# A decoder layer that reads its input transposed as well, with the gates' products ahead of the first norm's row

## The chip, the cores and the metric

The kernel runs on one core of a Trainium2 chip. The metric is the device time of one execution in microseconds (us). Three executions of the kernel before took 700.8, 701.33 and 701.66 us; the median is 701.33 us. Engines: TensorE (PE, its weight loads PEld) multiplies, VectorE (DVE), ScalarE (ACT) and GpSimd (POOL) do the rest, SyncE (SP) and ACT issue DMAs.

## What is computed

One layer of a decoder on x of 256 tokens by 1024 columns. In the reference's words, cut:

```python
xn = rmsnorm(h, mix_norm_g)          # x * rsqrt(mean(x*x) + eps) * g
proj = xn @ w_in                     # aq ak av | mq mk mv mo | mi mf | ga gm
ya = moba_attention(aq, ak, av)
qk = silu(causal_dwconv(concat(mq, mk), conv_w) + conv_b)
ym = mlstm_chunkwise(q, k, mv, mi + b, mf + b)   # gates i, f: 4 heads each
h = h + (sigmoid(ga) * (ya @ w_up_attn) + sigmoid(gm) * (ym @ w_up_mlstm)) @ w_out
h = h + hierarchical_moe(rmsnorm(h))             # 32 experts, top 2 per token
h = rmsnorm(h + (p @ w_ple_proj) * sigmoid(rmsnorm(h) @ w_ple_gate))
```

The change touches only what comes first: the norm of x, the projections mq, mi and mf, mk and aq, and the small vectors (gains, biases, the convolution's weights).

## The kernel before

All arithmetic is 32-bit. A large product is made of three of TensorE's fast kind: each operand is split into a rounded part (`whi`, written by ACT) and the rest (`wlo`, written by DVE: operand minus `whi`), and hi*hi, hi*lo and lo*hi are summed in PSUM. So every 128x512 piece of a weight costs ACT one pass, DVE one pass and TensorE 12 products of 128x256. The pieces pass through three staging buffers (`whi`, `wlo`), later two more (`spare`), so ACT may run up to three pieces ahead of TensorE. The tokens' scale 1/rms is not multiplied into x: the products use x times the gain, and the scale is applied to the results (`rT`, the scales as a row on every partition).

Weights arrive by DMA in 2 MB slots of a ring of ten; XT (x transposed, split, 8 blocks of 128 columns), RW, QK and VV hold results in slots of the same ring. A slot is refilled when its last reader is done. After the front come 32 experts of 6 MB each through the same ring, then a gate product and the last norm.

The start: SP issues x in two halves (L76) between the four 512 KB pieces of the mq weights (L77), then six small vectors, each into some rows of one tile (L92), the gates' weights and biases (L100 to L103), and then the 2 MB weights mk, aq, ak, av, mv, mo (L108). Each DMA uses one of eight completion counters in turn, and its issue waits until the DMA that had that counter before has landed. TensorE runs NWARM0 = 3 products on the identity (L231, `pw`), transposes x with 16 products (L257, `pt`), and for each block k of x runs 12 products into `pmq` (L308 to L310). ACT writes XT and `whi` (L299, L305), DVE their rests (L300, L306), and ACT sums the squares of x in four passes among them (L278). The row `rT` is made from the scales by two transposes (L285, `prt`) ahead of block 6. Then follow a transpose of the small vectors (L246, `pcol`), the gates' 24 products into `pif` (L331 to L333), the chain of small operations on the gates (L396 to L410, `scratch`), the transposes of its result (L416, `pam`), and the products of mk and aq (L331 to L333, `po`), whose results DVE scales by `rT` (L543, L548, L372). The convolution (L362 to L368) follows on ACT and DVE.

The Tile framework orders the instructions on each engine when the program is built; each engine then runs its own in that order, and `after(a, b)` adds an edge that puts a behind b on its engine.

Of the kernel before, what the change touches and what calls it, by code (L numbers as in the profile page):

```python
# [8 lines left out]
F32 = mybir.dt.float32  # L9
# [9 lines left out]
P = 128  # L19
T = 256  # L20
NB = 2
# [13 lines left out]
NWARM0 = 3  # L35
# [13 lines left out]
def layer(ctx: ExitStack, tc: tile.TileContext, A, dbg=None):  # L49
# [13 lines left out]


# [15 lines left out]
    rows = fc.tile([76, P], F32, name="rows")  # L80
    col_of = {}
    r0 = 0
    for nm, src in (
            ("g2", A["ffn_norm_g"].rearrange("o (k p) -> (o k) p", p=P)),
            ("g3", A["ple_norm_g"].rearrange("o (k p) -> (o k) p", p=P)),
            ("cb", A["conv_b"].rearrange("o (k p) -> (o k) p", p=P)),
            ("cw", A["conv_w"].rearrange("o c (k p) -> (o c k) p", p=P)),
            ("gml", A["mlstm_norm_g"].rearrange("o (k p) -> (o k) p", p=P)),
            ("bg", A["b_gate"].rearrange("o (k p) -> (o k) p", p=P)),
    ):  # L90
        n = src.shape[0]
        nc.sync.dma_start(out=rows[r0:r0 + n], in_=src)  # L92
        col_of[nm] = r0
        r0 += n

    wif = fc.tile([P, KD, 8], F32, name="wif")
    ifb = fc.tile([36, 1], F32, name="ifb")

    def load_if():
        nc.sync.dma_start(out=wif, in_=A["w_if"])  # L100
        ifb_v = A["mlstm_if_b"].rearrange("o n -> n o")
        nc.sync.dma_start(out=ifb[0:4], in_=ifb_v[0:4])
        nc.sync.dma_start(out=ifb[32:36], in_=ifb_v[4:8])  # L103
# [13 lines left out]
    first_act = nc.scalar.activation(identb, ident, AF.Copy)  # L117
# [20 lines left out]
    for nm in ("mk", "aq", "ak", "av", "mv", "mo"):  # L138
        wts[nm] = load_cols(A["w_mix"][MIX.index(nm)])
# [66 lines left out]
    def load_router():  # L206
# [6 lines left out]
        nc.sync.dma_start(out=rb[:, 0:NG], in_=A["router_group_b"].to_broadcast([P, NG]))  # L213
        nc.sync.dma_start(out=rb[:, 8:], in_=A["router_expert_b"].to_broadcast([P, NE]))
# [29 lines left out]
    def load_columns():  # L244
        pcol = psf.tile([P, 512], F32, name="pcol", tag="tp")
        nc.tensor.transpose(pcol[:, 0:76], rows, ident[0:76, 0:76])  # L246
        nc.vector.tensor_copy(out=cols, in_=pcol[:, 0:76])
        nc.vector.tensor_scalar(bgh, cols[:, col_of["bg"]:col_of["bg"] + 16], 0.5, None, op0=OP.mult)

# [3 lines left out]
    def transpose_x(k):  # L253
        pt = psf.tile([P, 2, T], F32, name="pt", tag="tp")
        for kk in range(2):
            for b in range(NB):
                after(nc.tensor.transpose(pt[:, kk, b * P:(b + 1) * P], h[:, b, (k + kk) * P:(k + kk + 1) * P], ident),  # L257
                      warm0)
        return pt

    ss = small.tile([P, 2, NB], F32, name="ss", bufs=1)
# [3 lines left out]
    seq = {"act": first_act, "dve": g1_copy}  # L265
# [5 lines left out]
    def on_dve(ins):  # L271
        after(ins, seq["dve"])
        seq["dve"] = ins

    def square_x(i):
        for b in range(NB):
            cs = slice(i * 512, (i + 1) * 512)
            on_act(nc.scalar.activation(y[:, b, cs], h[:, b, cs], AF.Square, accum_out=ss[:, i, b:b + 1]))  # L278

    def norm_x():  # L280
        nc.vector.tensor_tensor(ss[:, 0], ss[:, 0], ss[:, 1], op=OP.add)
        rstd_of(r1[:, 0:NB], ss[:, 0], D, NB)
        prt = psf.tile([P, 512], F32, name="prt", tag="at", bufs=3)
        for b in range(NB):
            nc.tensor.transpose(prt[:, b * P:(b + 1) * P], r1[:, b:b + 1].to_broadcast([P, P]), ident)  # L285
        nc.vector.tensor_copy(out=rT, in_=prt[:, 0:T])
        nc.vector.tensor_scalar(r1[:, 2:4], r1[:, 0:NB], 0.5, None, op0=OP.mult)

    pts = {}
    for k in range(KD):  # L290
        if k in (0, 2, 3):
            for kt in {0: (0, 2), 2: (4,), 3: (6,)}[k]:
                pts[kt] = transpose_x(kt)
# [810 lines left out]
```

## Time and profile before

| | us |
|---|---|
| median of three executions | 701.33 |
| the profiled execution | 701.26 |
| its span, first to last instruction | 699.6 |
| outside the span | 1.66 |
| TensorE busy in the span | 556.4 |
| DVE busy | 279.4 |
| ACT busy | 187.4 |
| mean granted clock of TensorE | 0.925 |

Busy time is a mean over stages with different limits. The front (0 to about 220 us) is one stage, the experts (to about 660 us) another, the end a third; what a change in the front is worth has to be read there, and then followed to the end.

### The profile page before, as it was taken

The page shows a single profiled execution, that of the slowest core. Times are in us where ns is not written, and L with a number is a line of the kernel's source. Part 1 is how long each engine was busy: PE and PEld are TensorE (multiplying, and loading weights), DVE is VectorE, ACT ScalarE, POOL GpSimd, SP SyncE. Part 2 cuts the span into 40 slices and gives each one's busy share as a digit, 9 for nine tenths or more (in the row PEclk, how much of TensorE's full clock was granted, in tenths as well). Part 3 has the DMA queues.
Part 4 walks back from the last instruction along what each step waited for, and adds up shares of the span by engine and source line. Part 5 has one row for each costly group of instructions (what it writes and reads, how often), then busy time and mean ns, then how long its engine had stood idle before and what let it go on. Part 6 is the DMA issues. An engine that isn't in the chain of part 4 may idle for free.

```text
span 699.6 us, 12231 instructions
## 1 busy us (share of the span) xinstructions
PE 556.4 (80%) x5165; PEld 378.1 (54%) x5165; DVE 279.4 (40%) x685; ACT 187.4 (27%) x426; POOL 34.6 (5%) x56
## 2 busy tenths in 40 slices
PE   7899999999999998595566655967656985865895
PEld 6799778899986554252233222634323442432374
DVE  5898667676665333041122015313211230310174
ACT  6575556465453211000000000010000210000164
POOL 3000000001300000000000000000000000000061
PEclk9999999999999999799799787999978997798999
DMA  7956533338787799999999999999999999999911
GB/s 257 430 221 260 219 122 121 121 121 331 301 340 301 316 430 421 433 423 428 427 425 429 426 429 421 427 428 422 430 425 425 424 427 427 428 426 427 412 63 61
DMA packets 21993, 241.49 MB, mean 345 GB/s; under 512 B 4694, under 2 KB 5290, under 8 KB 6955
## 3 DMA queue, kind: packets, MB, share of 16 engines
q1 hardware_dynamic: 21770, 240.37, 82.9%
q8 instruction: 42, 0.69, 0.4%
q10 hardware_dynamic: 160, 0.27, 0.1%
q14 instruction: 21, 0.16, 0.1%
HBM read 239.58 MB, written 1.05 MB: 344 GB/s over the span
## 4 chain that ended last, share of the span: by engine, by line
DMA 49%; PE 44%; DVE 3%; ACT 2%; issue 2%; POOL 1%; POOLq 0%; DVEq 0%; ACTq 0%; SPq 0%
DMA wt<-in_expert_gu 37%; DMA wt<-in_expert_down 11%; PE pg L811 5%; PE po L331 4%; PE po L333 4%; PE po L332 4%; PE po L348 2%; PE po L347 2%; PE po L349 2%; PE px L762 2%; PE pd L828 2%; PE ps L840 2%; PE ps L924 1%; PE pyy L471 1%; PE G L1014 1%
## 5 line engine op out<-in xcount | busy, mean ns | idle before, releaser
L811 PE MATMUL pg<-wt,xe 128*32 128x256 f32 x2032 | 150.6, 431 | 72.5 <-DMA wt<-in_expert_gu 72.5
L811 PEld LDWEIGHTS pg<-wt,xe 128*32 128x32 f32 x2032 | 72.2, 120 | 136.2 <-DMA wt<-in_expert_gu 54.8
L828 PE MATMUL pd<-wt,hT 128*32 128x256 f32 x1024 | 75.4, 443 | 22.0 <-DMA wt<-in_expert_down 17.9
L834 DVE COPY eo<-pd 32x256 f32<-32x256 f32 x64 | 27.1, 423 | 112.7 <-ACT eo L836 112.6
L828 PEld LDWEIGHTS pd<-wt,hT 128*32 128x32 f32 x1024 | 38.7, 124 | 47.4 <-issue 33.3
L836 ACT ACTIVATE eo<-pd 32x256 f32<-32x256 f32 x64 | 23.9, 374 | 147.9 <-PE pd L828 132.5
L221 DVE TENSOR_TENSOR wlo<-wt,whi 128x512 fp32r<-128x512 f32 x76 | 51.6, 686 | 19.5 <-ACT whi L220 19.3
L817 DVE TENSOR_TENSOR hid<-sg,pg 128x128 f32<-128x128 f32 x32 | 9.2, 287 | 122.9 <-ACT sg L815 122.9
L220 ACT ACTIVATE whi<-wt 128x512 fp32r<-128x512 f32 x77 | 47.1, 626 | 32.1 <-PE po L349 14.4
L815 ACT ACTIVATE sg<-pg 128x128 f32<-128x128 f32 x32 | 8.9, 277 | 168.9 <-PE pg L811 168.8
L762 PE MATMUL px<-og,y 128*128 128x128 f32 x256 | 38.4, 302 | 10.8 <-DVE og L753 7.4
L762 PEld LDWEIGHTS px<-og,y 128*128 128x128 f32 x256 | 34.3, 210 | 23.0 <-issue 11.4
L333 PE MATMUL po<-XT,wlo 128*128 128x256 f32 x144 | 40.7, 282 | 1.6 <-DVE wlo L221 1.6
L331 PE MATMUL po<-XT,whi 128*128 128x256 f32 x144 | 40.7, 282 | 0.2 <-ACT whi L220 0.2
L332 PE MATMUL po<-XT,whi 128*128 128x256 f32 x144 | 40.3, 280 | 0.0
L766 DVE TENSOR_TENSOR xe<-px,cols 128x256 f32<-128x256 f32 x32 | 13.6, 425 | 66.0 <-PE pg L811 42.2
L840 PE MATMUL ps<-eo,dwT 128*128 128x512 f32 x64 | 31.6, 613 | 5.9 <-DVE eo L834 5.8
L221 POOL TENSOR_TENSOR glo<-wt,ghi 128x1024 fp32r<-128x1024 f32 x4 | 10.6, 2657 | 446.7 <-DMA wt<-in_w_ple_gate 445.9
L333 PEld LDWEIGHTS po<-XT,wlo 128*128 128x128 f32 x144 | 27.1, 188 | 2.3 <-DVE wlo L221 2.2
L331 PEld LDWEIGHTS po<-XT,whi 128*128 128x128 f32 x144 | 27.1, 188 | 0.4 <-ACT whi L220 0.4
L332 PEld LDWEIGHTS po<-XT,whi 128*128 128x128 f32 x144 | 27.2, 189 | 0.2 <-issue 0.2
L221 DVE TENSOR_TENSOR spare<-wt,spare 128x512 fp32r<-128x512 f32 x34 | 23.3, 688 | 9.9 <-ACT spare L220 9.8
(374 smaller groups left out, 949.6 us busy)
## 6 DMA issues: line engine op xcount, KB each, us to landing
wt<-in_expert_gu SPq DMA_DIRECT2D x63, 2048.0 KB, 38.5
wt<-in_expert_down SPq DMA_DIRECT2D x30, 2048.0 KB, 39.1
wt<-in_w_mix SPq DMA_DIRECT2D x10, 2048.0 KB, 22.1
wt<-in_w_up SPq DMA_DIRECT2D x2, 2048.0 KB, 8.4
wt<-in_w_out SPq DMA_DIRECT2D x2, 2048.0 KB
wt<-in_expert_down SPq DMA_DIRECT2D x4, 1024.0 KB
wt<-in_w_ple_gate SPq DMA_DIRECT2D x4, 1024.0 KB, 27.1
wt<-in_w_mix SPq DMA_DIRECT2D x4, 512.0 KB, 7.1
```

The lines of the kernel that those rows point to most:

```text
L220: a = nc.scalar.activation(dst_hi, src, AF.Copy)
L221: b = (lo_on or nc.vector).tensor_tensor(dst_lo, src, dst_hi.bitcast(F32), op=OP.subtract)
L331: mm(out[:, f], whi[:, kk], ahi[:, k], start=(k == 0), stop=False)
L332: mm(out[:, f], whi[:, kk], alo[:, k], start=False, stop=False)
L333: mm(out[:, f], wlo[:, kk], ahi[:, k], start=False, stop=(k == kn - 1))
L347: mm(outs[b], ahi[:, k, bs], whi[:, k - k0], start=(k == 0), stop=False)
L762: ins = mm(px[:, k], y[:, b, kc:kc + P], og[:, b], start=(b == 0), stop=(b == NB - 1))
L811: ins = pe(mm(pg[32 * j:32 * j + 32], xe[:, k, 32 * i:32 * i + 32], gu[k][:, :, j * P:(j + 1) * P], start=(k == 0), stop=(k == KD - 1)))
L828: pe(mm(pd[32 * c:32 * c + 32], hT[:, 32 * j:32 * j + 32], dn[j][:, c * 256:(c + 1) * 256], start=(j == 0), stop=(j == 3)))
L834: nc.vector.tensor_copy(out=dst, in_=pd[32 * c:32 * c + 32])
L836: nc.scalar.activation(dst, pd[32 * c:32 * c + 32], AF.Copy)
L840: mm(ps, dwT[0:n, b], eo[0:n, c * 512:(c + 1) * 512], start=True, stop=True)
```

## The change

Inputs: the host also lays out x transposed (`xT`, 128 partitions by 8 blocks by 256 tokens) and all small vectors as columns of one array (`cols`, 128 by 85, the gates' biases in the last column). The kernel loads `cols` and then `xT` in blocks of 1, 1, 2 and 4 on ACT's queue, into QK's slot, while SP loads the mq weights in the same steps. Natural x follows on SP in one piece, then mk in two halves. The transposes of x, of the gain and of the vectors go. The squares of x are summed behind all eight blocks of the mq product, in two passes; the gates' 24 products come next, and the two transposes for `rT` behind them. mk and aq run ahead of the transposes of the gates' result (`pam`), and the two spare staging buffers come in behind aq. NWARM0 is 7, and the identity in bf16 is written by DVE instead of ACT.

```diff
-NWARM0 = 3
+NWARM0 = 7
-    g1r = fc.tile([KD, P], F32, name="g1r")
-    nc.scalar.dma_start(out=g1r, in_=A["mix_norm_g"].rearrange("o (k p) -> (o k) p", p=P))
+    NC_ = 85
+    cols = const.tile([P, NC_], F32, name="cols")
+    nc.scalar.dma_start(out=cols, in_=A["cols"])
+    QK = slot([P, 2, 8, T], F32, name="QK")
+    aqk, qkc = QK[:, 0], QK[:, 1]
     wts = {"mq": slot([P, KD, 512])}
     mq_v = A["w_mix"][MIX.index("mq")]
-    for i in range(4):
-        if i < 2:
-            nc.sync.dma_start(out=h[:, :, i * 512:(i + 1) * 512], in_=x_v[:, :, i * 512:(i + 1) * 512])
-        nc.sync.dma_start(out=wts["mq"][:, 2 * i:2 * i + 2], in_=mq_v[:, 2 * i:2 * i + 2])
+    for k, n in ((0, 1), (1, 1), (2, 2), (4, 4)):
+        nc.scalar.dma_start(out=aqk[:, k:k + n], in_=A["xT"][:, k:k + n])
+        mq_load = nc.sync.dma_start(out=wts["mq"][:, k:k + n], in_=mq_v[:, k:k + n])
...
-    first_act = nc.scalar.activation(identb, ident, AF.Copy)
+    nc.vector.tensor_copy(out=identb, in_=ident)
...
     load_if()
-    for nm in ("mk", "aq", "ak", "av", "mv", "mo"):
+    h_load = nc.sync.dma_start(out=h, in_=x_v)
+    after(h_load, mq_load)
+    wts["mk"] = slot([P, KD, 512])
+    for k in range(0, KD, 4):
+        nc.sync.dma_start(out=wts["mk"][:, k:k + 4], in_=A["w_mix"][MIX.index("mk")][:, k:k + 4])
+    for nm in ("aq", "ak", "av", "mv", "mo"):
...
     def norm_x():
-        nc.vector.tensor_tensor(ss[:, 0], ss[:, 0], ss[:, 1], op=OP.add)
-        rstd_of(r1[:, 0:NB], ss[:, 0], D, NB)
...
+        for b in range(NB):
+            on_act(nc.scalar.activation(y[:, b], h[:, b], AF.Square, accum_out=ss[:, b:b + 1]))
+        rstd_of(r1[:, 0:NB], ss, D, NB)
+
+    def norm_row(behind):
+        prt = psf.tile([P, 512], F32, name="prt", tag="tp")
+        for b in range(NB):
+            after(nc.tensor.transpose(prt[:, b * P:(b + 1) * P], r1[:, b:b + 1].to_broadcast([P, P]), ident), behind)
...
-        xt, g = pts[k // 2 * 2][:, k % 2], g1c[:, k:k + 1]
+        xt, g = aqk[:, k], col("g1", k)
...
-    load_columns()
+    norm_x()
...
-        pif = psf.tile([P, 2, T], F32, name="pif", tag="po", bufs=3)
-        proj_T(lambda k, f: wif32[:, k:k + 4], KD, 1, x_hi, x_lo, pif)
+        pif = psf.tile([P, 2, T], F32, name="pif", tag="at", bufs=3)
+        last_mm = proj_T(lambda k, f: wif32[:, k:k + 4], KD, 1, x_hi, x_lo, pif)
+        norm_row(last_mm)
+        for f in range(4):
+            nc.vector.tensor_tensor(raw[:, f, 3:], pmq[f], rT, op=OP.mult)
...
-    for f in range(4):
-        nc.vector.tensor_tensor(raw[:, f, 3:], pmq[f], rT, op=OP.mult)
     if_gates()
+    chunk_T(wts["mk"], evac_raw(4))
+    chunk_T(wts["aq"], evac_q)
     last_exp = if_columns()
-    chunk_T(wts["mk"], evac_raw(4))
     spare["tile"] = keep.tile([P, 2, 2, 512], F32R, name="spare", tag="y")
-    chunk_T(wts["aq"], evac_q)
```

The first DMAs that SP issues, before: h is natural x, wt the mq weights, rows the small vectors, wif and ifb the gates' weights and biases.

```order
L76 DMA h<-in_x 128x2x512
L77 DMA wt<-in_w_mix 128x1024
L76 DMA h<-in_x 128x2x512
L77 DMA wt<-in_w_mix 128x1024 x3
L92 DMA rows<-in_ffn_norm_g 8x128
L92 DMA rows<-in_ple_norm_g 8x128
L92 DMA rows<-in_conv_b 8x128
L92 DMA rows<-in_conv_w 32x128
L92 DMA rows<-in_mlstm_norm_g 4x128
L92 DMA rows<-in_b_gate 16x128
L100 DMA wif<-in_w_if 128x64
```

The same place on SP now; the sizes 512, 512, 1024 and 2048 are the mq weights, the two of 2048 behind h are mk.

```order
L86 DMA wt<-in_w_mix 128x512 x2
L86 DMA wt<-in_w_mix 128x1024
L86 DMA wt<-in_w_mix 128x2048
L90 DMA wif<-in_w_if 128x64
L122 DMA h<-in_x 128x2x1024
L126 DMA wt<-in_w_mix 128x2048 x2
L95 DMA wt<-in_w_mix 128x4096 x5
```

Natural x moved behind the mq weights, and nine small DMAs that stood between mq and mk are one (wif).

ACT's first instructions before, up to the third block: XT is the rounded part of x times the gain, scratch takes the squares.

```order
L69 DMA g1r<-in_mix_norm_g 8x128
L117 ACT_TABLE_LOAD
L117 ACTIVATE identb<-ident 128x128
L299 ACTIVATE XT<-pt,g1c 128x256
L305 ACTIVATE whi<-wt 128x512
L299 ACTIVATE XT<-pt,g1c 128x256
L305 ACTIVATE whi<-wt 128x512
L278 ACTIVATE scratch,ss<-h 128x512 x2
L299 ACTIVATE XT<-pt,g1c 128x256
```

ACT's first instructions now; QK holds x as it arrives transposed.

```order
L75 DMA cols<-in_cols 128x85
L85 DMA QK<-in_xT 128x256 x2
L85 DMA QK<-in_xT 128x512
L85 DMA QK<-in_xT 128x1024
L230 ACT_TABLE_LOAD
L230 ACTIVATE r_187<-mhalf 128x8
L255 ACTIVATE XT<-QK,cols 128x256
L261 ACTIVATE whi<-wt 128x512
L255 ACTIVATE XT<-QK,cols 128x256
L261 ACTIVATE whi<-wt 128x512
```

Five DMA issues stand ahead of the table load and the first pass instead of one, and the squares are no longer among the first blocks; they stand behind the eighth.

TensorE around the transposes of the gates' result, before: po here is the end of mk's sixth piece of eight.

```order
L331 MATMUL po<-XT,whi 128x256
L332 MATMUL po<-XT,whi 128x256
L416 MATMUL pam<-ident,scratch 128x36 x2
L333 MATMUL po<-XT,wlo 128x256
L331 MATMUL po<-XT,whi 128x256
L332 MATMUL po<-XT,whi 128x256
```

TensorE behind the gates' products now: po is mk's first piece.

```order
L288 MATMUL pif<-XT,whi 128x256
L289 MATMUL pif<-XT,whi 128x256
L290 MATMUL pif<-XT,wlo 128x256
L249 MATMUL prt<-ident,r_187 128x128 x2
L288 MATMUL po<-XT,whi 128x256
L289 MATMUL po<-XT,whi 128x256
L290 MATMUL po<-XT,wlo 128x256
```

The two transposes for the row stand behind the gates' products, and the wait on the gates' chain (`pam`) has moved out of mk to behind all 96 products of aq.

## Rows read from the trace of the kernel before

**Rows 1.** Busy time by stage: us, then engine busy (instructions), clock, DMA share, GB/s

```profile
22.60:38.50 15.90, 12.57 (x99) 11.54 (x99) 12.75 (x29) 9.84 (x18) 1.36 (x2) 1.00 1.01 430
50.00:150.00 100.00, 99.67 (x663) 83.64 (x662) 69.97 (x170) 56.53 (x134) 3.32 (x5) 1.00 0.42 156
200.00:660.00 460.00, 333.00 (x3615) 184.42 (x3613) 115.79 (x337) 51.94 (x140) 0.70 (x1) 0.89 0.98 414
```

**Rows 2.** The chain that ended last, by engine

```profile
DMA 49%; PE 44%; DVE 3%; ACT 2%; issue 2%; POOL 1%; POOLq 0%; DVEq 0%; ACTq 0%; SPq 0%
```

**Rows 3.** SP's waits from 20 to 260 us: waited for, us, times, longest

```profile
SPq L713 <- DVE wlo L221: 20.2, 3, 12.1
```

**Rows 4.** The first instructions of SP, ACT and TensorE: start, us, what, idle before

```profile
0.92 0.60 ACTq L69 DMA_DIRECT2D g1r<-in_mix_norm_g  x1
1.56 1.28 ACT L117 ACT_TABLE_LOAD   x1 [1.56 <-PEq L1094]
3.21 1.46 PE L231 MATMUL pw<-identb 128*128 128x512 bf16 x3 [3.21 <-ACT identb L117]
5.23 1.94 PE L257 MATMUL pt<-ident,h 128*128 128x128 f32 x8 [0.35 <-DMA h<-in_x]
6.43 0.47 ACT L299 ACTIVATE XT<-pt,g1c 128x256 fp32r<-128x256 f32 x1 [3.27 <-PE pt L257]
6.85 0.63 ACT L305 ACTIVATE whi<-wt 128x512 fp32r<-128x512 f32 x1
7.51 0.69 DVE L306 TENSOR_TENSOR wlo<-wt,whi 128x512 fp32r<-128x512 f32 x1
7.62 0.36 PE L308 MATMUL pmq<-XT,whi 128*128 128x256 f32 x1 [0.46 <-ACT whi L305]
8.35 0.62 ACT L278 ACTIVATE scratch<-h 128x512 f32<-128x512 f32 x1
10.44 0.60 PE L257 MATMUL pt<-ident,h 128*128 128x128 f32 x4
```

**Rows 5.** The same view: issues of mk and of the first experts, first gates' and mk products

```profile
12.65 5.93 SPq L108 DMA_DIRECT2D wt<-in_w_mix  x6
19.82 0.37 PE L331 MATMUL pif<-XT,whi 128*128 128x256 f32 x1
22.64 0.28 PE L331 MATMUL po<-XT,whi 128*128 128x256 f32 x1
160.00 5.47 SPq L713 DMA_DIRECT2D wt<-in_expert_gu  x2
```

**Rows 6.** Busy time in the first 15 us, columns as in rows 1

```profile
2.00:6.00 4.00, 2.44 (x8) 1.24 (x9) 0.17 (x1) 1.15 (x2) 2.15 (x14) 1.00 0.95 257
6.00:11.00 5.00, 4.54 (x36) 4.20 (x35) 3.06 (x6) 4.54 (x12) 0.00 (x0) 1.00 1.02 411
12.00:15.00 3.00, 3.00 (x28) 3.00 (x28) 2.54 (x7) 3.00 (x9) 1.15 (x2) 1.00 0.59 100
```

**Rows 7.** Line 77, the four DMAs of the mq weights

```profile
L77 SPq DMA_DIRECT2D wt<-in_w_mix x4: 452/587/710, 1.4 to 3.7; - x4
DMA to landing us min/median/max: 5.4/7.1/7.8
```

**Rows 8.** DVE and TensorE inside mk, columns as in rows 4

```profile
34.33 0.67 DVE L221 TENSOR_TENSOR wlo<-wt,whi 128x512 fp32r<-128x512 f32 x1
35.46 0.28 PE L416 MATMUL pam<-ident,scratch 36*128 36x36 f32 x2 [1.46 <-DVE scratch L410]
35.67 0.39 PE L333 MATMUL po<-XT,wlo 128*128 128x256 f32 x1
38.64 0.28 PE L331 MATMUL po<-XT,spare 128*128 128x256 f32 x1
```

**Rows 9.** TensorE after a long idle time among the experts, columns as in rows 4

```profile
435.50 6.19 PE L762 MATMUL px<-og,y 128*128 128x128 f32 x32 [7.35 <-DVE og L753]
```

**Rows 10.** Busy time while it runs: us, PE busy, clock, DMA share, GB/s

```profile
440.00:441.00 1.00, 1.00 (x9) 0.76 0.88 377
```

More of the change, by code (lines that the diff above doesn't have):

```diff
@@ L62, in slot, with after @@
         return ring.tile(shape, dt, name=name, tag="ring")
+    def after(a, b):
+        tc.add_manual_dep(a.ins, b.ins.name, mybir.DependencyInfo(
+            mybir.DependencyClass.NoSync, mybir.DependencyReason.DATA), reason="order on the engine")
     h = keep.tile([P, NB, D], F32, name="h")
@@ L67, in layer @@
     x_v = A["x"].rearrange("o (b p) d -> p (o b) d", p=P)
[L68 to L69 removed]
+    NC_ = 85
+    cols = const.tile([P, NC_], F32, name="cols")
+    nc.scalar.dma_start(out=cols, in_=A["cols"])
+    col_of = dict(g1=0, g2=8, g3=16, cb=24, cw=32, gml=64, bg=68)
+    ifb = cols[0:36, 84:85]
+    QK = slot([P, 2, 8, T], F32, name="QK")
+    aqk, qkc = QK[:, 0], QK[:, 1]
     wts = {"mq": slot([P, KD, 512])}
     mq_v = A["w_mix"][MIX.index("mq")]
[L74 to L94 removed]
+    for k, n in ((0, 1), (1, 1), (2, 2), (4, 4)):
+        nc.scalar.dma_start(out=aqk[:, k:k + n], in_=A["xT"][:, k:k + n])
+        mq_load = nc.sync.dma_start(out=wts["mq"][:, k:k + n], in_=mq_v[:, k:k + n])
     wif = fc.tile([P, KD, 8], F32, name="wif")
[L97 removed]
     def load_if():
[L100 to L103, printed above, removed]
+        after(nc.sync.dma_start(out=wif, in_=A["w_if"]), mq_load)
     def load_cols(v):
@@ L242, in col @@
         return cols[:, col_of[nm] + i:col_of[nm] + i + 1]
[L244 to L248, printed above, removed]
-    pmq = [psf.tile([P, T], F32, name="pmq", tag="po" if f < 3 else "at", bufs=3) for f in range(4)]
[L253 to L261, printed above, removed]
+    pmq = [psf.tile([P, T], F32, name="pmq", tag="po" if f < 3 else "at", bufs=3) for f in range(4)]
+    ss = small.tile([P, NB], F32, name="ss", bufs=1)
     r1 = small.tile([P, 8], F32, name="r1", bufs=1)
     rT = fc.tile([P, T], F32, name="rT")
-    seq = {"act": first_act, "dve": g1_copy}
+    seq = {"act": nc.scalar.activation(r1, mhalf, AF.Square), "dve": None}
     def on_act(ins):
@@ L310, in layer @@
             mm(pmq[f], wlo[:, f], x_hi[:, k], start=False, stop=(k == KD - 1))
-    load_columns()
+    norm_x()
+    on_dve(nc.vector.tensor_scalar(bgh, cols[:, col_of["bg"]:col_of["bg"] + 16], 0.5, None, op0=OP.mult))
     spare = dict(tile=None, n=0)
@@ L332, in proj_T @@
                     mm(out[:, f], whi[:, kk], alo[:, k], start=False, stop=False)
-                    mm(out[:, f], wlo[:, kk], ahi[:, k], start=False, stop=(k == kn - 1))
+                    ins = mm(out[:, f], wlo[:, kk], ahi[:, k], start=False, stop=(k == kn - 1))
+        return ins
     def proj_N(wt, ahi, alo, outs, mid=None):
@@ L1073, in cols @@
         return w.reshape(-1, P, w.shape[1] // n, n).transpose(2, 1, 0, 3)
+    a["xT"] = a["x"][0].T.reshape(KD, P, T).transpose(1, 0, 2)
+    vecs = [a.pop(nm).reshape(-1, P) for nm in ("mix_norm_g", "ffn_norm_g", "ple_norm_g", "conv_b", "conv_w",
+                                                "mlstm_norm_g", "b_gate")]
+    a["cols"] = _np.zeros((P, 85), _np.float32)
+    a["cols"][:, 0:84] = _np.concatenate(vecs).T
+    ifb = a.pop("mlstm_if_b").reshape(2, HM)
+    a["cols"][0:HM, 84], a["cols"][32:32 + HM, 84] = ifb[0], ifb[1]
     w_in = a.pop("w_in")[0]
```

44 lines of the change are left out of this document (10 added, 34 removed).

## The prediction

> **What bounds the kernel.** I read the busy time by stage first, then the chain, then the waits of the queue that issues the weights. Among the experts the DMA engines are busy 0.98 of the time at 414 GB/s while TensorE works 333 of 460 us [rows 1], and DMA is the largest part of the chain [rows 2]. So the middle runs at the pace of the expert weights, which the change does not touch. The front is different: from 50 to 150 us TensorE is busy 99.67 of 100 us and the DMA engines 0.42 [rows 1]. The two are tied by the ring: the first expert loads wait for DVE to finish splitting front weights (20.2 us over three waits [rows 3]), and DVE there follows TensorE's staging buffers. So a microsecond won before 50 us should be kept by TensorE up to the first expert load, start the whole stream earlier, and reach the end undiminished. What counts is when TensorE gets past the changed part, which ends with mk's last product.
>
> In that part two waits show. TensorE begins its first real product at 7.62 us, after x (0.5 MB, issued at 0.93) let the transposes start at 5.23 [rows 4]. And between the first mk product, 22.64, and the first aq product, 38.64 [rows 5, 8], it is busy only 12.57 of 15.9 us [rows 1].
>
> **The change, step by step.**
>
> *Length of the mq product.* From 7.62 to the first gates' product at 19.82 [rows 4, 5] are 12.2 us. In it stand two groups of four transposes, some 0.35 us each between their neighbours (starts 10.44 to about 10.8, [rows 4]), and about 0.35 us for `prt` and `pcol`. That leaves 11.1 us for 96 products, 0.115 us each. The gates' 24 products take 22.64 - 19.82 = 2.8 us [rows 5].
>
> *When it can start, by ACT.* ACT now issues five DMAs before its table load. One cost 0.60 there [rows 4], and SP's of this kind 0.45 to 0.71 [rows 7]; 0.92 + 0.60 + 4 x 0.55 is 3.7. The table load (1.28) ends at 5.1, a small Square at 5.3, then XT 0.47 and `whi` 0.63 give 6.35, DVE's `wlo` 0.69 [rows 4] gives 7.1. TensorE's order is now hi, lo, hi per column group, so the third product waits for `wlo`; that is as if the product started at 6.95 without a wait. Alone this would end the mq product at 6.95 + 11.1 = 18.05, 1.8 us ahead of 19.82.
>
> *When it can go on, by DMA.* Block 4 waits for the last 1 MB of mq. Ahead of and with it go 2.1 MB of mq, 1.05 MB of xT and 0.04 of `cols`: 3.19 MB. Before, 257 GB/s for 4 us and 411 for 5 moved 3.08 MB by 11.0 [rows 6], so 3.19 are moved at 11.3. Data landed later than it was moved in order: 0.52 MB of x at 257 GB/s is moved at 4.0, and PE could start at 5.23; the last mq piece, issued at 3.7, landed 7.8 later, 11.5 [rows 7], hardly after the queue ran dry. Here natural x and mk follow at once, so I take a lag of 0.8: landed at 12.1, with bounds 11.5 and 13.0. ACT 0.63, DVE 0.69 and the handovers put the third product of block 4 at 13.55, and the remaining 48 products (5.5 us, less the two already done) end at 18.85. So DMA, not ACT, sets the end of mq, and up to 0.8 us of any late start is hidden behind it. Gain at the first gates' product: 19.82 - 18.85 = 1.0.
>
> One row shows the DMA engines already 0.95 busy from 2 to 6 us with a single queue at work, and 1.02 after it [rows 6], so I give the second queue no bandwidth of its own. The Trainium skill says the same against the change's "beside" (DMA: Bandwidth & Descriptors, "Issuing engines are not separate DMA queues"): another issuing engine saves only issue time, since all run on the same DMA engines. Were it otherwise, xT would cost mq nothing, ACT would set the end at 18.05, and the gain would be 0.8 us larger.
>
> *Squares.* Two passes of 1024 instead of four of 512: 4 x 0.62 was the price [rows 4], now about 2 x 1.05 in ACT's order between the eighth `whi` (about 15.4) and the gates' first `whi`. That one is done near 18.1 and its rest on DVE near 18.8, just as TensorE arrives at 18.85: hidden, with about 0.3 us of cover. If natural x came after 15.4 the cover would go and TensorE would wait by as much; its 1.05 MB follow mq and are moved by about 13.9.
>
> *Row rT.* Its two transposes add 0.25 behind the gates. First mk product: 18.85 + 2.8 + 0.25 = 21.9 against 22.64: 0.75 won so far. mk itself is no longer late: its issue at 12.65 stood behind small DMAs that each waited for a large one, and the DMA engines moved only 100 GB/s from 12 to 15 [rows 5, 6]. Now mk follows x without a hole and lands by 20.
>
> *mk and the gates' chain.* TensorE idled 1.46 us for `pam` [rows 8]. With that wait behind aq, the next thing late is the seventh piece's `wlo`, done at 34.33 + 0.67 = 35.0 [rows 8], so its third product could have come at 35.05 instead of about 36.15: 1.1 won. Against it, the chain on DVE now starts about 3 us behind the first mk product, 1.8 before, and DVE's rests of mk still queue behind its links: I walk through waits of about 4 us in mk, 4.9 before (38.64 - 22.64 less 11.1). I take 0.9, with bounds 0 (the chain's waits just move) and 1.7 (the whole `pam` wait and its transposes). Behind aq `pam` is long ready; without the spare buffers aq runs on three, which is two pieces, 2.7 us, ahead against 1.3 us of ACT and DVE work: nothing.
>
> *The rest.* Four more `pw` at 0.49 each (1.46 for three [rows 4]) fill time in which TensorE has nothing to do. The small DMAs that vanish were off the path.
>
> Sum: 0.75 + 0.9 = 1.65 us. The profiled execution took 701.26, 699.6 of it in the span, 0.07 under the median; I forecast 701.33 - 1.65 = 699.7.
>
> **Rivals.**
>
> *A half-speed clock.* Three `pw` of 512 columns took 1.46 us, about 0.43 between starts, which is 1.2 GHz; the eight transposes at 5.23 also ran at half the pace of those at 10.44, and the first real product at 7.62 is the first at 2.4 [rows 4]. Now `pw` runs from about 2.0 to 5.1, and TensorE then idles until 6.4. If the clock is still at 1.2, products cost 0.214. From the first activity to full speed took about 4 us (3.21 to somewhat under 7.6); after the 7.35 us idle time in the experts, the clock rose around 440.5, 5 us after the start at 435.50 [rows 9, 10]. So 3 to 4 us of products at half pace lose 1.5 to 2 us; 0.8 of it hides behind the DMA: 0.7 to 1.2 lost, 700.6. For: the gap, and the stops while data comes. Against: seven `pw` without a gap. The Trainium skill (TensorE: Matmul & The Clock Gate, "What's actually happening") has the throttled clock as the default that activity releases; by that rule either outcome can come, and no row here has this gap.
>
> *The transfers come later (slower).* xT and the first mq blocks have rows of 1 and 2 KB. If they keep the 257 GB/s of the first 4 us [rows 6], 3.19 MB are moved at 14.4 and landed at 15.2, the mq product ends near 22 and mk starts near 25: 2.3 lost, 0.9 regained in mk, 702.8. It decides from a landing after about 13.9. Against: x's rows of 2 KB in the second half went through while the mean was 411 [rows 6].
>
> *ACT alone sets the start* (data by 11.3, a warm clock): 0.8 more, 698.9.
>
> *The front's gain is not passed on:* 701.3. Against it are the waits of the loads on DVE [rows 3].
>
> **Chances.** Likeliest case 0.50, 699.7, its own range 698.9 to 700.7; half-speed clock 0.23; ACT alone 0.12; not passed on 0.06; late transfers 0.09. A measurement of this kernel tells about 0.2%, 1.4 us. Faster by more than that (under 699.9): 0.32 of the likeliest, 0.12, and a little of the clock case, 0.46 together. Slower (over 702.7): 0.05 of the late transfers and 0.02 for what I did not see. Within: 0.47. Range: 698.7 (ACT alone with 0.2 more in mk) to 701.7 (nothing gained, and the spread of the runs above their median).
>
> **What the profile after would show.** Right: the third mq product near 7.1 at about 0.115 us per product; a stop of TensorE before block 4, for DMA, to about 13.5; the first gates' product near 18.9 without a wait, the first mk product near 21.9, the first aq product near 37; SP's first expert load 1.5 to 2 us before 160.00 [rows 5]. Wrong: products 0.21 us apart after 7 us (clock); block 4 after 15 (transfers); a wait of more than 0.5 us for the gates' `whi` (squares); the aq product no earlier against mk than before (chain); or all this early and the first expert load not.

## The result, and the profile after

The changed kernel takes **705.79 us** (median of 4, 705.49 to 707.28) where the kernel before took 701.41: a ratio of 1.0068 (95% interval 1.0056 to 1.008). It is slower by 4.4 us; the forecast was 1.65 us faster. The profiled execution took 705.66 us, 704.1 of it in the span.

TensorE's start and the end of the mq product (start, us, what, idle before and what ended it), which answer to [rows 4, 5]:

```profile
1.96 3.17 PE L215 MATMUL pw<-identb 128*128 128x512 bf16 x7 [1.96 <-DVE identb L104]
7.04 0.55 PE L264 MATMUL pmq<-XT,whi 128*128 128x256 f32 x1 [1.91 <-ACT whi L261]
...
10.61 0.41 PE L264 MATMUL pmq<-XT,whi 128*128 128x256 f32 x1
10.82 0.32 PE L265 MATMUL pmq<-XT,whi 128*128 128x256 f32 x1
10.98 0.28 PE L266 MATMUL pmq<-XT,wlo 128*128 128x256 f32 x1
...
13.97 0.28 PE L264 MATMUL pmq<-XT,whi 128*128 128x256 f32 x1
...
18.65 0.28 PE L264 MATMUL pmq<-XT,whi 128*128 128x256 f32 x1
...
20.45 0.28 PE L288 MATMUL pif<-XT,whi 128*128 128x256 f32 x1
```

The first product comes 0.58 us earlier than before, but from 8.05 until 10.82 the products are 0.213 us apart, 256 columns at 1.2 GHz (below: half pace). After that they are not back at the pace of before. From 13.97 to 18.65 stand 39 products, 0.120 us each. In the kernel before, the same stretch reads:

```profile
13.08 0.28 PE L308 MATMUL pmq<-XT,whi 128*128 128x256 f32 x1
...
16.48 0.28 PE L308 MATMUL pmq<-XT,whi 128*128 128x256 f32 x1
```

That is 30 products in 3.40 us, 0.1133 each. The gates start at 20.45 instead of 19.82.

Behind the gates, TensorE and then DVE, columns as above:

```profile
23.32 0.38 PE L249 MATMUL prt<-ident,r 128*128 128x128 f32 x2
25.31 0.35 PE L288 MATMUL po<-XT,whi 128*128 128x256 f32 x1 [1.61 <-DVE RW L352]
```
```profile
23.74 0.42 DVE L250 COPY rT<-prt 128x256 f32<-128x256 f32 x1 [0.42 <-PE prt L249]
24.08 0.16 DVE L251 TENSOR_SCALAR r<-r 128x2 f32<-128x2 f32 x1
24.15 0.69 DVE L205 TENSOR_TENSOR wlo<-wt,whi 128x512 fp32r<-128x512 f32 x1
24.75 1.41 DVE L352 TENSOR_TENSOR RW<-pmq,rT 128x256 f32<-128x256 f32 x4
```

The first mk product now waits 1.61 us for the first of the four scalings of `pmq` on DVE, because its `po` tile takes over a PSUM buffer that `pmq` held. Those scalings need `rT`, whose transposes now stand behind all gates' products. The mk product comes at 25.31; before it came at 22.64 [rows 5].

All waits of TensorE from its first mq product up to 70 us (us in total, times, longest), then the first load of the experts:

```profile
PE pmq L264 <- ACT whi L261: 1.9, 1, 1.9
PE po L290 <- DVE wlo L205: 1.8, 3, 1.1
PE po L288 <- DVE RW L352: 1.6, 1, 1.6
PE po L290 <- DVE spare L205: 0.7, 1, 0.7
```
```profile
163.48 0.34 SPq L672 DMA_DIRECT2D wt<-in_expert_gu  x1
```

The wait of 1.46 us for `pam` [rows 8] is gone; a new one of 0.7 stands in ak, on the spare tile. The experts' loads begin 3.48 us later than at 160.00 [rows 5], and 540.6 us pass from there to the end of the span, against 539.6 before. So in this trace 3.5 us are lost in the front and 1.0 in the stream.

Two differences are in no line of the diff as such. The first is in the weight loads of the products whose weights come from a staging buffer (a staged tile), in the front from 22 us on (duration in ns: least, median, most; first and last start), here and then in the kernel before:

```profile
L288 PEld LDWEIGHTS po<-XT,whi x152: 186/192/200, 25.3 to 163.8; 128*128 128x128 f32 x152
L288 PEld LDWEIGHTS po<-XT,spare x63: 187/188/218, 52.7 to 164.9; 128*128 128x128 f32 x63
```
```profile
L331 PEld LDWEIGHTS po<-XT,whi x144: 187/188/200, 22.5 to 164.5; 128*128 128x128 f32 x144
```

Those with a staged tile take 192 ns instead of 188, those with the spare tile 188 in both. The second is that tiles moved in SBUF: `cols`, 85 wide, takes 352 bytes per partition where it took 320, and four small tiles of the front (`rows`, `g1r`, `ifb`, `g1c`: 1088 bytes together) are gone. So the ring's slots, into which all weights are loaded, start 224 bytes above a multiple of 256 instead of 192; and `whi` and `wlo` stand, modulo 256, 0 bytes from XT instead of 64 (205280 - 167136 = 149 x 256; before 206336 - 183488 = 89 x 256 + 64). Below, this remainder is called the distance.

### The profile page after: what moved, and what is told of

Same layout as the page of the kernel before. It is cut to its first block, busy times and chain, and to the rows that moved or that the text cites. A ratio compares the mean times of both kernels' runs of the same rounds, so it can differ in the third digit from the quotient of the medians.

```text
span 704.1 us, 12180 instructions
## 1 busy us (share of the span) xinstructions
PE 561.0 (80%) x5151; PEld 381.9 (54%) x5151; DVE 281.7 (40%) x683; ACT 188.8 (27%) x422; POOL 33.7 (5%) x55
## 4 chain that ended last, share of the span: by engine, by line
DMA 49%; PE 44%; DVE 3%; ACT 2%; issue 1%; POOL 0%; POOLq 0%; ACTq 0%; DVEq 0%; SPq 0%
DMA wt<-in_expert_gu 33%; DMA wt<-in_expert_down 16%; PE pg L770 5%; PE po L290 4%; PE po L288 4%; PE po L289 4%; PE po L305 3%; PE po L306 3%; PE po L307 3%; PE ps L799 2%; PE pd L787 2%; PE px L721 2%; PE ps L883 1%; PE pyy L432 1%; PE pmq L264 1%
## 5 line engine op out<-in xcount | busy, mean ns | idle before, releaser
L770 PE MATMUL pg<-wt,xe 128*32 128x256 f32 x2032 | 153.3, 438 | 71.7 <-DMA wt<-in_expert_gu 71.7
L205 DVE TENSOR_TENSOR wlo<-wt,whi 128x512 fp32r<-128x512 f32 x78 | 54.0, 701 | 21.0 <-ACT whi L204 20.7
L204 ACT ACTIVATE whi<-wt 128x512 fp32r<-128x512 f32 x80 | 49.9, 630 | 44.4 <-PE po L289 23.0
L288 PE MATMUL po<-XT,whi 128*128 128x256 f32 x156 | 44.8, 287 | 1.6 <-DVE RW L352 1.6
L290 PE MATMUL po<-XT,wlo 128*128 128x256 f32 x156 | 44.3, 285 | 1.8 <-DVE wlo L205 1.8
L289 PE MATMUL po<-XT,whi 128*128 128x256 f32 x156 | 44.3, 284 | 0.0
L290 PEld LDWEIGHTS po<-XT,wlo 128*128 128x128 f32 x156 | 29.8, 191 | 2.4 <-DVE wlo L205 2.4
L288 PEld LDWEIGHTS po<-XT,whi 128*128 128x128 f32 x156 | 29.8, 191 | 1.9 <-issue 1.8
L289 PEld LDWEIGHTS po<-XT,whi 128*128 128x128 f32 x156 | 29.8, 191 | 0.2 <-issue 0.2
L801 DVE TENSOR_TENSOR h<-ps,h 128x512 f32<-128x512 f32 x32 | 22.1, 691 | 9.3 <-PE ps L799 9.3
```

The costliest lines, as they stand in the source:

```text
L204: a = nc.scalar.activation(dst_hi, src, AF.Copy)
L205: b = (lo_on or nc.vector).tensor_tensor(dst_lo, src, dst_hi.bitcast(F32), op=OP.subtract)
L288: mm(out[:, f], whi[:, kk], ahi[:, k], start=(k == 0), stop=False)
L289: mm(out[:, f], whi[:, kk], alo[:, k], start=False, stop=False)
L290: ins = mm(out[:, f], wlo[:, kk], ahi[:, k], start=False, stop=(k == kn - 1))
L770: ins = pe(mm(pg[32 * j:32 * j + 32], xe[:, k, 32 * i:32 * i + 32], gu[k][:, :, j * P:(j + 1) * P], start=(k == 0), stop=(k == KD - 1)))
```

## The experiments

All 13 were timed beside the kernel before, whose median was 701.0 to 701.4. The last columns are from each profiled execution, a single run that lies up to 1.7 us off its median: first load of the experts; from there to the end of the span.

| version | median us | ratio, 95% interval | first load | to the end |
|---|---|---|---|---|
| before | 701.3 | | 160.00 | 539.6 |
| change | 705.79 | 1.0056 to 1.008 | 163.48 | 540.6 |
| a_align | 701.44 | 0.9991 to 1.0008 | 163.26 | 537.5 |
| b_shift | 701.95 | 0.9995 to 1.0013 | 160.72 | 540.0 |
| a_align_warm | 700.74 | 0.9985 to 1.0002 | 163.00 | 536.3 |
| a_align_row | 700.03 | 0.9971 to 0.9988 | 162.78 | 536.4 |
| a_rel64 | 699.74 | 0.9971 to 0.9991 | 163.47 | 536.1 |
| b_rel0 | 703.43 | 1.0019 to 1.0039 | 162.34 | 540.1 |
| b_ring256 | 697.52 | 0.9934 to 0.9961 | 160.88 | 536.1 |
| a_ring128 | 705.12 | 1.0043 to 1.0071 | 164.63 | 540.2 |
| a_psum | 697.56 | 0.993 to 0.9957 | 161.27 | 536.4 |
| a_psum_warm | 697.24 | 0.9933 to 0.996 | 158.88 | 535.7 |
| best | 696.84 | 0.9917 to 0.9944 | 158.99 | 536.7 |
| b_best | 697.98 | 0.9936 to 0.9963 | 161.38 | 535.8 |
| a_pam_back | 699.98 | 0.998 to 0.9999 | 163.12 | 536.3 |

### First, the 32 bytes

My first theory was that operands 32 bytes off a multiple of 64 slow every engine. **a_align**, the changed kernel with:

```
-    cols = const.tile([P, NC_], F32, name="cols")
-    nc.scalar.dma_start(out=cols, in_=A["cols"])
+    cols = const.tile([P, 96], F32, name="cols")
+    nc.scalar.dma_start(out=cols[:, 0:NC_], in_=A["cols"])
```

> The changed kernel with the tile of columns made 96 wide in memory instead of 85 (the 85 are loaded as before), so that every tile allocated behind it starts 32 bytes later, as in the kernel before: the ten large buffers, the stage tiles and the work tiles at multiples of 64 bytes. Theory 1 (the slower time is mostly these 32 bytes: TensorE, VectorE and ScalarE work slower on operands that start 32 bytes off a multiple of 64): products 0.114 us apart instead of 0.120, the products with a staged tile 276 ns and those with the spare tile 280, wlo on VectorE 686 ns instead of 701, first load of the experts near 160 us, about 4.4 us less than the changed kernel: 701.4 us (701.0 to 702.3). Theory 2 (the new order, its wait for a PSUM buffer and the clock cost it all): nothing changes, 705.8 us (705.3 to 706.3), products 0.120 apart.

**b_shift**, the kernel before with one more constant tile:

```
+    pad = const.tile([P, 8], F32, name="pad")
+    nc.gpsimd.memset(pad, 0.0)
```

> The kernel before with one more tile of 32 bytes per partition among the constants (GpSimd clears it once), so that the large buffers, the stage and the work tiles start 32 bytes off a multiple of 64; nothing else differs. Theory 1 (alignment): products 0.120 us apart, 701.4 plus 3.5 to 4.5, 705.4 us. Theory 2 (the changed order is the cause): within 0.2% of the kernel before, 701.4 us, products 0.114 apart.

a_align came out at the expected 701.44, and for the wrong reason. Its products are still 0.120 us apart, its weight loads 192 ns, and the experts begin at 163.26, as late as ever; of the 3.3 us between the two traces, 3.1 were won in the 540 us behind that. b_shift, with its operands 32 bytes off, has loads of 188 ns and lies 0.6 us above before, an interval that contains no change. So the theory fell. Busy time from 300 to 600 us (last: DMA share, GB/s), of before, the change and a_align:

```profile
300.00:600.00 300.00, 203.80 (x2176) 107.56 (x2176) 67.85 (x191) 26.30 (x71) 0.00 (x0) 0.87 1.01 426
```
```profile
300.00:600.00 300.00, 203.10 (x2176) 107.65 (x2176) 68.46 (x192) 26.64 (x72) 0.00 (x0) 0.88 1.01 425
```
```profile
300.00:600.00 300.00, 205.50 (x2196) 108.76 (x2200) 68.38 (x192) 26.58 (x72) 0.00 (x0) 0.87 1.01 429
```

In a_align the ring starts at a multiple of 256, and the stream runs at 429 GB/s instead of 425. What slows the products had to be something that a_align shares with the change and b_shift with the kernel before. Two things are left: the order of the work, and the distance between staging buffers and ring.

### The clock and the norm's row

**a_align_warm** is a_align with more `pw`:

```
-NWARM0 = 7
+NWARM0 = 13
```

> The aligned version with 13 products on pw ahead of the first real product instead of 7, so that TensorE works on until that product is ready. If TensorE's half clock at the start (17 products 0.21 us apart) comes from the idle time before the first product, products are 0.114 apart from the first on; block 4 of the first weights (landed near 12.6 us) then shows as a wait of 0.5 to 1 us, and the first gates' product comes at 18.8 to 19.4 instead of 20.2. Theory 1: 0.5 to 1.2 us under the aligned version, near 700.5. Rival: the half clock lasts a fixed time whatever stands before it, the six more products only delay the first real one by 0.5 us or more, and the time is that of the aligned version or up to 0.6 above.

**a_align_row** is a_align with the row behind the first 12 of the gates' 24 products:

```
-        last_mm = proj_T(lambda k, f: wif32[:, k:k + 4], KD, 1, x_hi, x_lo, pif)
-        norm_row(last_mm)
+        proj_T(lambda k, f: wif32[:, k:k + 4], KD, 1, x_hi, x_lo, pif, mid=norm_row)
...
```

> The aligned version with the first norm's row (two transposes, its copy on VectorE and what scales pmq by it) put after the first 12 of the 24 gates' products instead of behind all of them. Theory (the first mk product waits 1.6 us because its PSUM buffer is released by the scaling of pmq, which needs that row): the wait goes, the first mk product comes 1.3 to 1.6 us earlier, and if it is passed on 1.0 to 1.5 us come off, near 700.2. Rival: VectorE, which must do wlo for mk and the four scalings in the same stretch, hands the wait on to wlo of the next mk blocks, and the time is within 0.3 us of the aligned version.

With 13 `pw`, which last until the first product is ready, no product of the start runs at half pace:

```profile
1.96 5.39 PE L215 MATMUL pw<-identb 128*128 128x512 bf16 x13 [1.96 <-DVE identb L104]
6.99 0.47 PE L264 MATMUL pmq<-XT,whi 128*128 128x256 f32 x1
7.30 0.28 PE L265 MATMUL pmq<-XT,whi 128*128 128x256 f32 x1
7.42 0.28 PE L266 MATMUL pmq<-XT,wlo 128*128 128x256 f32 x1
```

The gates came at 20.01 instead of 20.26, not near 19: TensorE now stopped at block 1 (0.51 us for `whi`, 0.22 for `wlo`), because ACT waited for that block of xT; the half pace had hidden it. The median fell by 0.7, within the expectation; the intervals overlap, but 10 of its 12 runs lie under 701.1 and only one of a_align's. In a_align_row the wait on `RW` shrank from 1.61 to 0.19 us and the time by 1.4, as expected. In its trace the gates began 0.9 later, at 21.20, since in that execution the half pace lasted until 12.9, and the first mk product only 0.5 earlier.

### Distance between operands, start of the rows

**a_rel64** is a_align with one more tile in the front's constants:

```
+    fpad = fc.tile([P, 16], F32, name="fpad")
+    nc.gpsimd.memset(fpad, 0.0)
     rb = fc.tile([P, 8 + NE], F32, name="rb")
```

> The aligned version with one more tile of 64 bytes per partition among the front's constants: the large buffers stay where they are (multiples of 256 bytes), the stage tiles move up by 64, so that the weights of a product (whi, wlo) and what it multiplies (XT, YS) stand 64 bytes apart modulo 256, as in the kernel before (206336 - 183488 = 22848), and not 0 (205312 - 167168 = 38144, which is 149 times 256). Theory 1 (products slow down when both operands have the same address modulo 256): products from the stage 0.1133 us apart instead of 0.120, those from the spare tile 0.1167 as in all kernels so far, the first load of the experts at about 160 instead of 163.3 us, and the time 2.5 to 3.5 us under the aligned version's 701.4, near 698.5. Rival (the slower products come from the other order, not from addresses): 0.120 apart, 701.4.

**b_rel0** is the kernel before with the same tile, wider:

```
+    fpad = fc.tile([P, 48], F32, name="fpad")
+    nc.gpsimd.memset(fpad, 0.0)
     rb = fc.tile([P, 8 + NE], F32, name="rb")
```

> The kernel before with one more tile of 192 bytes per partition among the front's constants, so that stage tiles and large buffers stand 0 bytes apart modulo 256, as in the changed kernel; the large buffers don't move and the order of the work is that of before. Theory 1: products from the stage 0.120 us apart instead of 0.1133, some 560 of them in the front, so up to 3.7 us; 2.5 to 3.7 us slower, 703.8 to 705.0. Rival (the order): 701.4, 0.1133 apart.

**b_ring256** is the kernel before with a constant tile as in b_shift, twice as wide:

```
+    pad = const.tile([P, 16], F32, name="pad")
+    nc.gpsimd.memset(pad, 0.0)
```

> The kernel before with one more tile of 64 bytes per partition among the constants, so that the large buffers, into which the weights are loaded, start at multiples of 256 bytes (before: 192 above one); stage and large buffers keep their distance. Theory (the loads run faster into rows that start at such multiples: 430 GB/s against 426 between 300 and 600 us in the traces of the aligned version and of the kernel before): the front as before, first load of the experts at 160 us, the stream of about 450 us at 430, so 3 to 4 us off at its end, near 698. Rival (the higher rate of the aligned version has another cause, the order of the loads for one): 701.4, 426 GB/s.

**a_ring128** is a_align with:

```
-    cols = const.tile([P, 96], F32, name="cols")
+    cols = const.tile([P, 128], F32, name="cols")
```

> The changed kernel with the tile of columns 128 wide in memory, so that the large buffers start 128 bytes above a multiple of 256. If the loads want multiples of 128, 430 GB/s and the time of the aligned version, 701.4; if they want 256, 426 GB/s and 704.8; the products stay 0.120 apart either way, since stage and large buffers still stand 0 bytes apart modulo 256.

Weight loads of a_rel64 and of b_rel0, columns as above:

```profile
L290 PEld LDWEIGHTS po<-XT,whi x152: 186/188/201, 26.6 to 163.6; 128*128 128x128 f32 x152
```
```profile
L333 PEld LDWEIGHTS po<-XT,whi x140: 187/192/201, 25.2 to 162.7; 128*128 128x128 f32 x140
```

The distance decides, in either order of the work. In a_rel64, 104 products from 39.64 to 51.45 are 0.1136 us apart; in b_rel0, 72 from 22.62 to 31.24 are 0.1197. In all six traces with a distance of 0, whose rings start 0, 128, 192 and 224 bytes above a multiple of 256, the staged products of the front stand 0.1195 to 0.120 apart in the mean. The time follows: 1.70 us won, 2.15 lost.

Both are under the 2.5 that I expected at least. Part of the reason is that at a distance of 64 bytes the products are not always 0.1133 apart. In a_rel64, 60 products between the two lines below stand 0.1177 apart, and in the kernel before 24 from 128.16 on stand 0.118 apart:

```profile
26.80 0.28 PE L291 MATMUL po<-XT,whi 128*128 128x256 f32 x1
...
33.86 0.28 PE L291 MATMUL po<-XT,whi 128*128 128x256 f32 x1
```

Over all staged products up to 165 us that follow one another without a stop, the mean is 0.1153 in a_rel64 and 0.1151 in before, against 0.1197 in a_align and b_rel0. At 0.0045 for some 560 products that is an estimate of 2.5 us, where the expectation had up to 3.7. What switches between the two paces is open. In a_rel64's trace the gain does not reach the experts: their first load comes at 163.47, where a_align has 163.26 and the expectation had 160. This execution ran at half pace from 9.30 to 15.3, a_align's only to 10.5. From the first mk product to that load it took 136.9 us, a_align's 138.1.

The start of the rows decides the stream, by itself. Every version with the ring at a multiple of 256 needs 535.7 to 537.5 us from the experts' first load to the end; with 128, 192 or 224 above one it needs 539.6 to 540.6. b_ring256 won 3.80 us over the kernel before by one unused tile of 64 bytes. The Trainium skill (DMA: Bandwidth & Descriptors, "How a descriptor splits into AXI transactions") says of reads that when a descriptor does not start on a 256-byte boundary, its first transaction starts at the boundary below, and the bytes before the start are fetched for nothing. The traces show a loss on the side that is written here, 425 to 426 GB/s against 429 to 430; whether it has the same cause no run tells.

### What the order itself costs

a_rel64 and b_ring256 have the same distance and the same start of rows, the one with the change's order, the other with that of before: 699.74 and 697.52. **a_psum** is a_rel64 with other PSUM buffers:

```
-    pmq = [psf.tile([P, T], F32, name="pmq", tag="po" if f < 3 else "at", bufs=3) for f in range(4)]
+    pmq = [psf.tile([P, T], F32, name="pmq", tag="at" if f < 3 else "po", bufs=3) for f in range(4)]
-        pif = psf.tile([P, 2, T], F32, name="pif", tag="at", bufs=3)
+        pif = psf.tile([P, 2, T], F32, name="pif", tag="po", bufs=3)
```

> The aligned version with 64 bytes between stage and large buffers (699.74 us), and pmq and pif put elsewhere in PSUM: three of the four pmq tiles share the buffers of pw, the fourth and pif those of po, so that one buffer of po is free when the first mk product comes and it need not wait until pmq has been scaled by the first norm's row. Theory (that wait, 1.61 us, is most of what the new order itself costs: 699.74 against 697.52 for the kernel before with the same two distances): no wait of the first mk product, 1.2 to 1.6 us off, 698.1 to 698.5. Rival: the second half of mk or its wlo blocks on VectorE wait longer by as much, and the time stays within 0.4 us of 699.74.

**a_psum_warm** adds `NWARM0 = 13`.

> The same with 13 products on pw instead of 7 ahead of the first real one. If the half clock at the start costs 0.7 us in this version as in the aligned one (701.44 to 700.74), 0.5 to 0.9 us off, 697.5. Rival: without the PSUM wait the transfers of the first weights bound the stretch up to the gates, and nothing comes off.

**best** adds to that:

```
-    cols = const.tile([P, 96], F32, name="cols")
+    cols = const.tile([P, 120], F32, name="cols")
...
     y = keep.tile([P, NB, D], F32, name="scratch", tag="y")
+    kpad = keep.tile([P, 40], F32, name="kpad")
...
```

> The same, and the spare tile moved so that it too stands 64 bytes above a multiple of 256, the large buffers staying at multiples of 256. Theory (a product slows by how its two operands stand to each other modulo 256 bytes): products from the spare tile 0.1133 us apart instead of 0.1167, some 250 of them, 0.5 to 0.8 us off, 696.9. Rival: the spare tile's rate has another cause, 0.1167 and 697.5.

**b_best** is b_ring256 with the same `kpad`, and `pad` 40 wide.

> The kernel before with the large buffers at multiples of 256 bytes (697.52 us) and the spare tile 64 bytes above one, for comparison with the mended order of the change at the same distances. Theory: 0.5 to 0.9 us under 697.52, 696.8, so that the change's order with its wait and its clock mended is worth nothing measurable (within 0.5 us). Rival: the mended order is worth the 1 to 1.6 us that the forecast gave it, and this kernel is slower than that by as much.

In a_psum the wait on `RW` is gone, and 2.18 us with it, more than the 1.61 of the wait:

```profile
24.74 0.38 PE L251 MATMUL prt<-ident,r 128*128 128x128 f32 x2
24.88 0.36 PE L290 MATMUL po<-XT,whi 128*128 128x256 f32 x1
```

So without its PSUM wait the change's order is worth nothing that these runs show: 697.56 against 697.52, of five runs each that spread over 2.7 and 1.3 us. Both traces have a stretch at half pace before 16 us. With 13 `pw` the first mk product comes at 22.39, the first of av at 59.68 and the experts at 158.88; in the trace of before, the one trace of its order without the half pace, at 22.64, 60.67 and 160.00. In the median that is only 0.3 us, which these five runs don't tell from nothing. In best, products with the spare tile are 0.1133 us apart late in the front (24 from 159.56 to 162.17) as expected, but 0.1178 early in it (24 from 57.03 to 59.74), so the expectation holds in part. Its time is the lowest, 696.84. The 0.4 to a_psum_warm can't be told from nothing, and b_best won nothing over b_ring256. Best is faster than the kernel before by 0.7%. Against b_best's 697.98 it is 1.14 us faster, and the ranges of the runs almost part (up to 697.34, from 697.30). That is what the rival of b_best's expectation said, but the two don't differ by the order alone: in b_best's trace most staged products up to 60 us are 0.1178 apart, in best's most are at 0.1133, at the same distance. So whether the mended order is worth up to 1 us or nothing stays open.

### The move of pam

**a_pam_back** is a_psum_warm with the old place:

```
+    last_exp = if_columns()
     chunk_T(wts["mk"], evac_raw(4))
+    spare["tile"] = keep.tile([P, 2, 2, 512], F32R, name="spare", tag="y")
     chunk_T(wts["aq"], evac_q)
-    last_exp = if_columns()
-    spare["tile"] = keep.tile([P, 2, 2, 512], F32R, name="spare", tag="y")
```

> The version with the two distances, the PSUM buffers and 13 pw mended (697.24 us), and the transposes pam with what they release put back ahead of the aq products, so that the spare tile is in use from aq on as in the kernel before, and not from ak on. The forecast took the move for 0.9 us won in mk and nothing lost behind aq. The trace of the version with 13 pw shows aq and ak with a cost of their own: pam between aq and ak (0.45 us in which no product starts) and a wait of 0.76 us for the rest of the first spare piece. Theory 1 (the move hands on what it wins): the first av product stands as far behind the first mk product as there, 37.3 us within 0.4, and the time is 697.2 within 0.5. Theory 2 (the forecast): 0.9 us longer, 698.1. Theory 3: the pam wait now hides behind the mk waits and ak's wait goes, 0.7 to 1.2 us shorter, 696.3.

It lost 2.74 us, so theory 2 had the sign and not the size. TensorE around `pam`, and the busy time from 38 to 45 (the third number from the end is the granted clock):

```profile
36.34 0.31 PE L379 MATMUL pam<-ident,scratch 36*128 36x36 f32 x2 [1.02 <-DVE scratch L373]
36.58 0.38 PE L292 MATMUL po<-XT,wlo 128*128 128x256 f32 x1
38.10 0.58 PE L290 MATMUL po<-XT,spare 128*128 128x256 f32 x1 [1.14 <-ACT spare L206]
38.48 0.41 PE L291 MATMUL po<-XT,spare 128*128 128x256 f32 x1
38.69 0.51 PE L290 MATMUL po<-XT,spare 128*128 128x256 f32 x1
39.55 0.58 PE L292 MATMUL po<-XT,spare 128*128 128x256 f32 x1 [0.35 <-POOL YS L130]
```
```profile
38.00:45.00 7.00, 6.55 (x29) 6.24 (x30) 4.80 (x9) 2.13 (x6) 1.41 (x2) 0.51 0.80 332
```

The stop for `pam` is followed by one for the spare tile, which can be written only when `pam` has read `scratch`, and then the granted clock is 0.51, 1.2 GHz, and products stand 0.21 us apart until about 44.6. Moving both behind mk and aq saves the two stops and that stretch. Not all of the difference between the two traces is `pam`'s: in a_pam_back's the staged products are 0.1178 apart from 10.31 to 31.80, where a_psum_warm's are at 0.1133, and its first mk product is 0.42 us later, ahead of the place of the edit.

## Why the prediction was wrong

The loss in steps that were each run: from the change to a_align 4.35 us, to a_rel64 1.70, to a_psum 2.18. On the other side, from the kernel before to b_ring256, 3.80. So the start of the rows made 0.55 of the 4.5 us of difference, the distance of the operands 1.70 (2.15 the other way round), the PSUM wait 2.18, and what is left is 0.04. Each step is known to about 1 us, so that the small rest is luck; the 0.55 can't be told from nothing, and neither can the 0.6 of b_shift, which moves the rows from 192 to 224. The 1.65 us that the sum had on the other side never came: with these causes taken away the two orders differ by 0.04 us in one pair (a_psum, b_ring256) and by 1.14 in the other (best, b_best), where the paces differ too.

**The length of a product.** The sum took 0.115 us from [rows 4, 5] as the price of a product in any order. It was 0.1133 to 0.114 there, and 0.120 after, because a distance of 64 bytes had become 0. I had read the tiles that the diff adds and drops, but not asked what moves behind them. Nothing in the profile of before could give the price, but the layout could have given a reason for a wider range.

**"First mk product: 18.85 + 2.8 + 0.25 = 21.9."** The step followed the row from TensorE to TensorE and left out the PSUM buffers. Before, `pif` took one of `po`'s buffers and `rT` was long ready; after, all three were held by `pmq` until DVE had `rT`. This is the wait that took the place of another, the thing to look for, and no rival of mine had it.

**"When it can start, by ACT."** The number came out, 7.04 against 6.95, by luck. ACT had done its table load and the small pass at 4.90, sooner than the 5.3 of the sum, and then waited for xT:

```profile
4.69 0.21 ACT L230 ACTIVATE r<-mhalf 128x8 f32<-128x8 f32 x1
5.87 0.51 ACT L255 ACTIVATE XT<-QK,cols 128x256 fp32r<-128x256 f32 x1 [0.96 <-DMA QK<-in_xT]
7.87 0.51 ACT L255 ACTIVATE XT<-QK,cols 128x256 fp32r<-128x256 f32 x1 [0.98 <-DMA QK<-in_xT]
```

So the transfers set the start and the second block, which the sum had only for block 4. Even in a_psum_warm, without the half pace and at 0.1133 per product, the first gates' product comes at 19.54, 0.28 us earlier than before and not 1.0.

**The clock.** The rival "a half-speed clock" came true: products 0.213 us apart from 7.04 to 10.82, after the idle time of 1.91 us. It is not most of what made the kernel slower: 13 `pw` take it away and win 0.7 us in one pair of versions and 0.3, which can't be told from nothing, in the other. I had also taken the trace of before for typical. It is full-paced from 7.62 on [rows 4], but its variants b_shift, b_rel0, b_ring256 and b_best, which only move tiles, run at half pace until 12 to 13. Which of the two the timed runs of before have stays open. In all nine variants whose trace has the half pace, the profiled execution is the slowest or second slowest of its version's runs; in three of the four with 13 `pw` it is not, nor in the change (third of four). That suggests that most timed runs lack it, and that these traces show more of it than the medians; no trace shows so.

**When it can go on, by DMA.** Block 4's `whi` started at 12.65 after a wait of 1.51 us for its data, so these landed near 12.6, inside my bounds of 11.5 and 13.0. The half pace hid it, as the rival said. But with 13 `pw`, where no half pace hides it, the stop stood before block 1.

**Squares.** Hidden, as the sum had it, but not at its times: the gates' `whi`, which it had done near 18.1, began on ACT at 18.82, and TensorE came at 20.45. Had TensorE come at 18.85, it would have waited.

**mk and the gates' chain.** The sign was right, the size not. From the first mk to the first aq product are 14.14 us in the change (25.31 to 39.45), before 16.00, so 1.86 were won where the sum had 0.9. Some of that comes from the late start alone: b_ring256, in the old order, starts mk at 25.35 and takes 14.42. "Behind aq `pam` is long ready; ... nothing" was wrong, since `pam` costs 0.45 us there and the spare tile 0.7. But the old place costs more in the new order: 2.7 us against my 0.9, two stops and a slow stretch where I had counted one stop.

**Handing on.** Right for the order of the change: from a_rel64 to a_psum the experts' first load came 2.20 us earlier, and the time fell by 2.18. But the 3.48 us at the experts are not simply the 2.67 by which the first mk product was late. The first aq product was late by only 0.81, and 2.67 were lost behind it, to `pam`, the spare tile and the slower products. And in the old order mk takes up most of a late start: in b_ring256's trace the first mk product comes 2.71 us later than in that of before, the first aq product 1.13, the experts' load 0.88.

**The stream.** The sum left it as it was. It was 1.0 us longer in the trace, 0.55 by the medians, which is within their noise.

## What to carry to other kernels

A diff that adds or drops a small tile moves every tile allocated behind it: compare start addresses before and after, first those of what long streams are loaded into, then the distance of a product's two operands. When an instruction is moved ahead of another, ask for each tile it writes who held that buffer last and what releases it. And before a gain is counted from one trace, ask whether its clock at the start is the usual one.

## What was unexpected of the hardware

- Two operands of a product at the same address modulo 256 bytes: 0.120 us between products of 256 columns and 192 ns for a weight load, against 188 ns and 0.1133 in some stretches, 0.1178 in others, at a distance of 64, and about 0.117 at 224 (the spare tile). Shown by a_rel64 and b_rel0; distances other than these three were not tried, and what chooses between the two paces at 64 is not known.
- Rows of weights that start at a multiple of 256 bytes: 429 to 430 GB/s and 3.8 us in 700, against 425 to 426 at 128, 192 or 224 above.
- At the start of the kernel the granted clock reads 1.00 while the spacing is that of 1.2 GHz, as here in the changed kernel:

```profile
7.00:10.80 3.80, 3.76 (x16) 3.63 (x17) 2.97 (x6) 2.93 (x7) 0.00 (x0) 1.00 1.01 402
```

The distance from start to start tells it, 16 products in 3.8 us. In a_pam_back, at 38 us, the same column does show it, and so it does in a_rel64, where TensorE had run at full pace from 7.60 to 8.57 and had then stopped before block 1:

```profile
9.30:15.20 5.90, 5.90 (x26) 5.68 (x27) 4.15 (x8) 3.61 (x8) 0.36 (x2) 0.50 1.03 426
```
